# One decoder layer on one core: the eight sums of query squares issued as one run, and the first weights moved to the queue that loads x

## The chip, the cores and the metric

The kernel runs on one core of a Trainium2 chip. The metric is device time in microseconds (us) of one execution, as the median of several runs. TensorE (PE in the rows) does the matmuls, VectorE (DVE) and ScalarE (ACT) the elementwise work, GpSimd (POOL) a little of it, and SyncE (SP) issues most of the DMAs. Times inside a profile count from the start of its span.

## The reference, cut to what matters

One layer of a hybrid decoder for 256 prompt tokens and 8 sampled tokens (264 columns in all), in float32:

```
proj = rms_norm(x, g_mix) @ w_in            # [q | k | v | z | xBC | dt]
q    = rms_norm per head of 64 (q, q_norm_g)
attn = sliding-window attention with sinks (q, k, v)
ssd  = Mamba-2 scan of xBC, dt, gated by silu(z)
x    = x + concat(attn, ssd) @ w_out
x    = x + cross-attention into 256 memory tokens
x    = x + ConvFFN(x)
```

For the change two pieces matter. The first is the opening: the first columns of `w_in` (k and v) times x, for which x (2048 features, 16 blocks of 128) and the weights must be loaded. The second is the norm of the queries: for 16 heads of 64 and 256 prompt tokens the sum of the squares over each head's 64 features.

## The kernel before, in words

Activations lie with features on the 128 partitions and the 264 tokens along the free axis. A projection is done in three matmuls per block of 128 features (lines 100 to 102): weights and activations are each split into a high part, rounded to the matmul's format, and a low remainder, and high x high, high x low and low x high are added in PSUM. The high parts are made by ScalarE (line 85 for weights), the low ones by VectorE (line 86). Each such matmul streams 264 (or 256) columns and is called a wide matmul here.

**The opening** (lines 187 to 261) is ordered by hand on SP, TensorE, ScalarE and VectorE. x and the first 512 weight columns come interleaved, block by block: a block k is 264 columns of x and 512 columns of weights. Block 0 comes in two DMAs, `open_x` (x of block 0 with the gain, 140 KB, issued by SP) and `open_w` (its weights, 256 KB, issued by ScalarE), then SP issues blocks 1 to 5 as one DMA each (388 KB) and blocks 6 to 15 two by two (776 KB). While these fly, TensorE does warm-up matmuls on zeros (line 201). For block 0, ScalarE makes the high part of x (line 161), VectorE and ScalarE each cast one half of the weights (lines 180, 181), VectorE makes the low part of x (line 165) and then that of the weights (line 184). TensorE does 12 matmuls a block (line 240): 4 column groups with high weights and high x, 4 with high weights and low x, 4 with low weights and high x. At the end of the opening come the matmuls for dt, 16 of 32 output columns (line 247), four column groups side by side.

**The query squares** (lines 601 to 631). The queries come out of four projections of two blocks each, eight blocks `qT[:, j]` in all. As each is ready, ScalarE squares it (line 611). Then eight matmuls with 32 output columns (line 615) sum the squares over each head: for d = 0, 1 and j = 0 to 3, block 4d + j adds into the partitions 32j to 32j + 31 of one PSUM bank `pq`, with a stationary matrix `nw[:, d]` that holds ones in the column of each head. The accumulation starts at d = 0 and stops at d = 1. In the profile each of these float32 matmuls is two passes. VectorE copies `pq` (line 628), TensorE transposes it, and from it the reciprocal norms of the queries are made for the attention.

Outside the opening, the order of instructions on each engine is worked out when the kernel is built, from estimated times and dependencies, with earlier lines first where several could go; `tc.high_priority()` puts some ahead, and `tc.issue_after(ins)` keeps the instructions of its block behind `ins` on the same engine. So the eight sums are set among the wide matmuls of the projections as their squares come free.

Of the kernel before, what the change touches and what calls it, by code (L numbers as in the profile page):

```python
# [16 lines left out]
TP, TS = 256, 8  # L17
T = TP + TS
# [29 lines left out]
def hybrid_decoder_step_kernel(ctx: ExitStack, tc: tile.TileContext, I, O):  # L48
    nc = tc.nc
    V, S, P, PE = nc.vector, nc.scalar, nc.gpsimd, nc.tensor  # L50
# [9 lines left out]
    def psum(tag):  # L60
        return ps.tile([128, 512], F32, tag=tag, name=tag, bufs=banks[tag])

    def T3(pool, n, dt=F32, tag=None, name=None, bufs=None):
        return pool.tile([128, n, T], dt, tag=tag, name=name or tag, bufs=bufs)
# [80 lines left out]
    BLK = T + 512  # L145
# [4 lines left out]
    def load(on, src, a, b, k):  # L150

        t = quarter[k // 4]
        o = t.shape[1] - 4 * BLK
        return on.dma_start(out=t[:, o + a:o + b], in_=src)

    def x_of(k):
        return blocks[k // 4][:, k % 4, 0:T], gmix[:, k:k + 1]

    def x_hi(k):
        x, g = x_of(k)  # L160
        return S.activation(out=A[k // 8][0][:, k % 8, :], in_=x, func=AF.Copy, scale=g)

    def x_lo(k):
        x, g = x_of(k)
        return V.scalar_tensor_tensor(out=A[k // 8][1][:, k % 8, :], in0=x, scalar=g, in1=A[k // 8][0][:, k % 8, :].bitcast(F32),
                                      op0=ALU.mult, op1=ALU.subtract)
# [10 lines left out]
    def w_split(k, n, half=False):  # L177
        raw, hi, lo = w_piece(k, n)
        if half:
            V.tensor_copy(out=hi[:, :, 0:256], in_=raw[:, :, 0:256])  # L180
            S.copy(out=hi[:, :, 256:512], in_=raw[:, :, 256:512])
        else:
            S.copy(out=hi, in_=raw)
        return lambda: V.tensor_tensor(out=lo, in0=raw, in1=hi.bitcast(F32), op=ALU.subtract)
# [9 lines left out]
    with tc.manual_schedule(engines={mybir.EngineType.SP, mybir.EngineType.PE, mybir.EngineType.Activation, mybir.EngineType.DVE}):  # L194
        V.memset(acc0, 0.0)
        load(nc.sync, I["open_x"], -KB, T, 0)
        load(S, I["open_w"], T, BLK, 0)

        S.activation(out=table, in_=acc0[:, 0:1], func=AF.Copy)
        for n in (T, T, T, 128):  # L200
            PE.matmul(warm[:, :n], acc0[:, 0:128], acc0[:, 0:n], start=True, stop=True)
        for k in range(1, 6):
            load(nc.sync, I["open_1"][k - 1], BLK * (k % 4), BLK * (k % 4 + 1), k)
        for k in range(6, KB, 2):
            load(nc.sync, I["open_2"][k // 2 - 3], BLK * (k % 4), BLK * (k % 4 + 2), k)

        squares = iter(range(4))

        def square():
            j = next(squares)  # L210
            S.activation(out=sw[j // 2][:, 4 * (j % 2):4 * (j % 2) + 4, :], in_=blocks[j][:, :, 0:T], func=AF.Square)
            if j % 2:
                w = sw[j // 2]
                V.tensor_tensor(out=w[:, 0:4, :], in0=w[:, 0:4, :], in1=w[:, 4:8, :], op=ALU.add)

        for k in range(6):
            x_hi(k)
            lo = w_split(k, 1, k < 2)
            x_lo(k)
            lo()  # L220
        for k in range(6, KB, 2):
            x_hi(k)
            x_hi(k + 1)
            lo = w_split(k, 2)
            x_lo(k)
            x_lo(k + 1)
            lo()
            if k >= 8:
                square()
        nc.sync.dma_start(out=wdt, in_=I["w_dt"])  # L230
        V.tensor_tensor(out=wdt, in0=wdt, in1=gmix.unsqueeze(2).broadcast_to([128, KB, 32]), op=ALU.mult)
        nc.sync.dma_start(out=cst, in_=I["cst"])
        nc.sync.dma_start(out=par, in_=I["par"])
        last_load = nc.sync.dma_start(out=hcol, in_=I["hcol"])

        def first_k(k, i):

            for x in range(2 - i):
                for c in range(4):
                    PE.matmul(first[c][:, :T], pre[k // 2][i][:, k % 2, c * 128:(c + 1) * 128], A[k // 8][x][:, k % 8, :],  # L240
                              start=k + i + x == 0, stop=k == KB - 1 and i == 1)

        def dt_round(r):

            for j in range(4):
                k = 4 * r + j
                PE.matmul(dt_ps[32 * j:32 * j + 32, :T], wdt[:, k, :], x_of(k)[0], start=r == 0, stop=r == 3)


        for ks in ((0,), (1,), (2,), (3,), (4,), (5,), *((k, k + 1) for k in range(6, KB, 2))):  # L250
            for i in range(2):
                for k in ks:
                    first_k(k, i)

        sq_last = S.activation(out=table, in_=sw[1][:, 7, 0:1], func=AF.Sqrt)
        V.tensor_tensor(out=sw[0][:, 0:4, :], in0=sw[0][:, 0:4, :], in1=sw[1][:, 0:4, :], op=ALU.add)
        V.tensor_tensor(out=sw[0][:, 0:2, :], in0=sw[0][:, 0:2, :], in1=sw[0][:, 2:4, :], op=ALU.add)
        add_last = V.tensor_tensor(out=acc0, in0=sw[0][:, 0, :], in1=sw[0][:, 1, :], op=ALU.add)
        for r in range(4):
            dt_round(r)  # L260
        sum_last = PE.matmul(sum0[:, :T], cst[:, C_ONE:C_ONE + 128], acc0, start=True, stop=True)
# [339 lines left out]
    qsq = [T3(apool, 4, tag="R", name=f"qsq{i}", bufs=4) for i in range(2)]  # L601
    nw = zz[:, :, 512:544]
# [7 lines left out]

            S.activation(out=qsq[j // 4][:, j % 4, :TP], in_=qT[:, j, :TP], func=AF.Square)
    pq = psum("s")
    for d in range(2):
        for j in range(4):
            PE.matmul(pq[32 * j:32 * j + 32, 0:TP], nw[:, d, :], qsq[d][:, j, :TP], start=d == 0, stop=d == 1)
    cpc = mp.tile([128, 24, 8], F32, name="cpc")
    ctmp = mp.tile([128, 2, TP], F32, tag="c", name="ctmp", bufs=2).rearrange("p a b -> p (a b)")[:, :192].rearrange("p (a b) -> p a b", b=8)

# [10 lines left out]
    pq = psum("x")  # L629
# [30 lines left out]
    for j in range(8):  # L660
        if j % 4 == 0:
            second_chunk(j // 4)
        d = 2 * (j // 4)
# [893 lines left out]
def build(shapes):  # L1557

    import concourse.bacc as bacc

    nc = bacc.Bacc("TRN2", target_bir_lowering=False, num_devices=1)
    ins = {n: nc.dram_tensor(f"in_{n}_dram", s, dt, kind="ExternalInput").ap() for n, (s, dt) in shapes.items()}
    outs = {n: nc.dram_tensor(f"out_{n}_dram", s, F32, kind="ExternalOutput").ap() for n, s in _OUTS}
    with tile.TileContext(nc, schedule_with_timeline_sim=True) as tc:
        hybrid_decoder_step_kernel(tc, ins, outs)
    return nc
# [10 lines left out]
```

## Time and profile before

| | us |
|---|---|
| median of 3 runs | 1399.48 (1399.35 to 1400.28) |
| the profiled execution, its own time | 1399.1 |
| its span, first to last instruction | 1396.8 |
| TensorE busy in the span | 1391.8 |
| VectorE busy | 1051.1 |
| ScalarE busy | 769.2 |
| GpSimd busy | 95.9 |

The granted clock of TensorE is full over the whole span. The span is what the views of the trace show; the profiled execution's own time has another 2.3 us around it. A row of a timeline gives the start, the length, the engine (q behind it: an issue by its sequencer), the line, the operation, what it writes and reads, the shape, how many like it follow each other, and in brackets how long the engine idled ahead of it and what ended that.

### The profile page before, as it was taken

The page shows a single profiled execution, that of the slowest core. Times are in us where ns is not written, and L with a number is a line of the kernel's source. Part 1 is how long each engine was busy: PE and PEld are TensorE (multiplying, and loading weights), DVE is VectorE, ACT ScalarE, POOL GpSimd, SP SyncE. Part 2 cuts the span into 40 slices and gives each one's busy share as a digit, 9 for nine tenths or more (in the row PEclk, how much of TensorE's full clock was granted, in tenths as well). Part 3 has the DMA queues.
Part 4 walks back from the last instruction along what each step waited for, and adds up shares of the span by engine and source line. Part 5 has one row for each costly group of instructions (what it writes and reads, how often), then busy time and mean ns, then how long its engine had stood idle before and what let it go on. Part 6 is the DMA issues. An engine that isn't in the chain of part 4 may idle for free.

```text
span 1396.8 us, 29012 instructions
## 1 busy us (share of the span) xinstructions
PE 1391.8 (100%) x11535; PEld 1366.9 (98%) x11535; DVE 1051.1 (75%) x1874; ACT 769.2 (55%) x1255; POOL 95.9 (7%) x286
## 2 busy tenths in 40 slices
PE   9999999999999999999999999999999999999999
PEld 8999999999999999899999999999999999999998
DVE  8879799999997774578777775777577757765654
ACT  7667756556545554566565544554455445543532
POOL 0000011121010000002010000000000000000000
PEclk9999999999999999999999999999999999999999
DMA  7954477777776577675676765676566656655654
GB/s 302 321 162 137 137 218 245 231 242 249 244 220 236 182 240 264 206 249 187 190 254 216 253 210 187 212 248 217 183 212 240 196 183 197 196 181 182 191 184 138
DMA packets 89479, 298.33 MB, mean 214 GB/s; under 512 B 12032, under 2 KB 17152, under 8 KB 88832
## 3 DMA queue, kind: packets, MB, share of 16 engines
q1 hardware_dynamic: 83696, 277.35, 60.9%
q0 software_dynamic: 5504, 18.88, 4.1%
q8 instruction: 90, 1.47, 0.4%
q14 instruction: 45, 0.37, 0.1%
q10 hardware_dynamic: 144, 0.26, 0.1%
HBM read 280.77 MB, written 16.23 MB: 213 GB/s over the span
## 4 chain that ended last, share of the span: by engine, by line
PE 99%; DMA 0%; ACT 0%; DVE 0%; issue 0%
PE mm L100 21%; PE mm L101 21%; PE mm L102 21%; PE t L100 10%; PE t L102 10%; PE t L101 10%; PE t L240 1%; PE y L825 1%; PE t L278 1%; PE y L841 0%; PE mm L240 0%; PE s L240 0%; PE x L278 0%; PE t L559 0%; PE x L1137 0%; DMA open<-in_open_x_dram 0%
## 5 line engine op out<-in xcount | busy, mean ns | idle before, releaser
L85 ACT CAST whi<-wraw 128x1024 fp32r<-128x1024 f32 x440 | 459.7, 1048 | 527.4 <-PE mm L101 277.7
L86 DVE TENSOR_TENSOR wlo<-wraw,whi 128x1024 fp32r<-128x1024 f32 x440 | 540.1, 1229 | 220.6 <-ACT whi L85 216.7
L100 PE MATMUL mm<-x2h,whi 128*128 128x264 f32 x704 | 199.9, 284 | 0.0
L100 PE MATMUL t<-x2h,whi 128*128 128x264 f32 x704 | 199.8, 284 | 0.0
L102 PE MATMUL t<-x2h,wlo 128*128 128x264 f32 x704 | 199.7, 284 | 0.0
L101 PE MATMUL mm<-x2l,whi 128*128 128x264 f32 x704 | 199.6, 284 | 0.0
L101 PE MATMUL t<-x2l,whi 128*128 128x264 f32 x704 | 199.5, 283 | 0.0
L102 PE MATMUL mm<-x2h,wlo 128*128 128x264 f32 x704 | 199.4, 283 | 0.0
L101 PE MATMUL mm<-hl,whi 128*128 128x264 f32 x704 | 198.7, 283 | 0.0
L102 PE MATMUL mm<-hh,wlo 128*128 128x264 f32 x704 | 198.2, 283 | 0.0
L100 PE MATMUL mm<-hh,whi 128*128 128x264 f32 x704 | 197.2, 284 | 0.0
L100 PE MATMUL mm<-xh,whi 128*128 128x264 f32 x576 | 164.7, 287 | 0.0
L101 PE MATMUL mm<-xl,whi 128*128 128x264 f32 x576 | 164.5, 287 | 0.0
L102 PE MATMUL mm<-xh,wlo 128*128 128x264 f32 x576 | 162.8, 287 | 0.0
L101 PEld LDWEIGHTS mm<-x2l,whi 128*128 128x128 f32 x704 | 132.5, 188 | 0.0
L101 PEld LDWEIGHTS t<-x2l,whi 128*128 128x128 f32 x704 | 132.5, 188 | 0.0
L100 PEld LDWEIGHTS t<-x2h,whi 128*128 128x128 f32 x704 | 132.5, 188 | 0.0
L100 PEld LDWEIGHTS mm<-x2h,whi 128*128 128x128 f32 x704 | 132.4, 188 | 0.1
L101 PEld LDWEIGHTS mm<-hl,whi 128*128 128x128 f32 x704 | 132.4, 188 | 0.0
L102 PEld LDWEIGHTS t<-x2h,wlo 128*128 128x128 f32 x704 | 132.2, 188 | 0.0
L102 PEld LDWEIGHTS mm<-x2h,wlo 128*128 128x128 f32 x704 | 132.1, 188 | 0.0
L102 PEld LDWEIGHTS mm<-hh,wlo 128*128 128x128 f32 x704 | 131.9, 188 | 0.0
(506 smaller groups left out, 2951.5 us busy)
## 6 DMA issues: line engine op xcount, KB each, us to landing
wraw<-in_w_up_dram SPq DMA_DIRECT2D x176, 512.0 KB, 4.4
wraw<-in_w_in_dram SPq DMA_DIRECT2D x96, 512.0 KB, 4.7
wraw<-in_w_dn_dram SPq DMA_DIRECT2D x88, 512.0 KB, 4.2
wraw<-in_w_out_dram SPq DMA_DIRECT2D x48, 512.0 KB, 4.3
h<-in_h_dram POOLq DMA_DIRECT2D x32, 256.0 KB, 4.7
hn<-in_h_dram SPq DMA_DIRECT2D x16, 512.0 KB, 5.0
out_state_s_dram<-hn POOLq DMA_DIRECT2D x16, 512.0 KB, 3.8
e<-dram_la SPq DMA_DIRECT2D x16, 256.0 KB, 5.1
```

The source lines that it names most:

```text
L85: S.copy(out=hi, in_=x)
L86: V.tensor_tensor(out=lo, in0=x, in1=hi.bitcast(F32), op=ALU.subtract)
L100: PE.matmul(out, wh, xh, start=start, stop=False)
L101: PE.matmul(out, wh, xl, start=False, stop=False)
L102: return PE.matmul(out, wl, xh, start=False, stop=stop)
L240: PE.matmul(first[c][:, :T], pre[k // 2][i][:, k % 2, c * 128:(c + 1) * 128], A[k // 8][x][:, k % 8, :], start=k + i + x == 0, stop=k == K ...
L278: return PE.transpose(out, in_, cst[0:k, C_ID:C_ID + k])
L825: PE.matmul(y[o:o + 64, (h // 2) * 128:(h // 2) * 128 + 128], xdt[:, h, :], es[h // 4][:, h % 4, :], start=True, stop=True)
```

## The change

The DMA of block 0's weights is issued by SP, between that of x and that of block 1, and no more by ScalarE. The eight sums of squares are issued in another order: first that of d = 1, j = 3 (the last block, whose squares come last), and behind it, by `issue_after`, the other three of d = 1 and then the four of d = 0. The accumulation starts at d = 1 and stops at d = 0.

```diff
         load(nc.sync, I["open_x"], -KB, T, 0)
-        load(S, I["open_w"], T, BLK, 0)
+        load(nc.sync, I["open_w"], T, BLK, 0)
...
     pq = psum("s")
-    for d in range(2):
-        for j in range(4):
-            PE.matmul(pq[32 * j:32 * j + 32, 0:TP], nw[:, d, :], qsq[d][:, j, :TP], start=d == 0, stop=d == 1)
+
+    def q_sums(d, j):
+        return PE.matmul(pq[32 * j:32 * j + 32, 0:TP], nw[:, d, :], qsq[d][:, j, :TP], start=d == 1, stop=d == 0)
+
+
+    with tc.issue_after(q_sums(1, 3).ins):
+        for d in (1, 0):
+            for j in range(4 if d == 0 else 3):
+                q_sums(d, j)
```

## Rows read from the trace of the kernel before

**Rows 1.** The page: busy time of the engines with their share of the span and instructions, and the shares of the chain of work that ended last.
```profile
PE 1391.8 (100%) x11535; PEld 1366.9 (98%) x11535; DVE 1051.1 (75%) x1874; ACT 769.2 (55%) x1255; POOL 95.9 (7%) x286
...
PE 99%; DMA 0%; ACT 0%; DVE 0%; issue 0%
```

**Rows 2.** The waits of TensorE over the whole span: who waited for whom, us in total, times, the longest.
```profile
PE x L201 <- DVE eps L274: 1.2, 1, 1.2
PE t L240 <- ACT xh L161: 0.5, 1, 0.5
```

**Rows 3.** The timeline of TensorE from 4 to 8.3 us: block 0 of the opening and the start of blocks 1 (6.79) and 2 (8.25).
```profile
5.10 0.48 PE L240 MATMUL t<-xh,whi 128*128 128x264 f32 x2 [0.46 <-ACT xh L161]
5.42 0.33 PE L240 MATMUL mm<-xh,whi 128*128 128x264 f32 x1
5.58 0.28 PE L240 MATMUL s<-xh,whi 128*128 128x264 f32 x1
...
6.19 0.51 PE L240 MATMUL t<-xh,wlo 128*128 128x264 f32 x2
6.54 0.29 PE L240 MATMUL mm<-xh,wlo 128*128 128x264 f32 x1
...
6.79 0.40 PE L240 MATMUL t<-xh,whi 128*128 128x264 f32 x2
...
8.25 0.28 PE L240 MATMUL t<-xh,whi 128*128 128x264 f32 x1
```

**Rows 4.** The timeline of ScalarE from 0 to 7.4 us: its issue of the first weights, and blocks 0 and 1.
```profile
0.74 0.41 ACTq L154 DMA_DIRECT2D open<-in_open_w_dram  x1
...
4.49 0.52 ACT L161 ACTIVATE xh<-open 128x264 fp32r<-128x264 f32 x1 [1.82 <-DMA open<-in_open_x_dram]
4.92 0.39 ACT L181 CAST whi<-open 128x256 fp32r<-128x256 f32 x1
5.63 0.52 ACT L161 ACTIVATE xh<-open 128x264 fp32r<-128x264 f32 x1 [0.33 <-DMA open<-in_open_dram]
```

**Rows 5.** The timeline of VectorE from 0 to 7.4 us: block 0 and the first cast of block 1.
```profile
4.66 0.29 DVE L180 CAST whi<-open 128x256 fp32r<-128x256 f32 x1 [3.50 <-DMA open<-in_open_w_dram]
5.04 0.49 DVE L165 SCALAR_TENSOR_TENSOR xl<-open,xh 128x264 fp32r<-128x264 f32 x1
5.45 0.68 DVE L184 TENSOR_TENSOR wlo<-open,whi 128x512 fp32r<-128x512 f32 x1
6.05 0.29 DVE L180 CAST whi<-open 128x256 fp32r<-128x256 f32 x1
```

**Rows 6.** The timeline of SP from the start: its first issues (the second row merges ten).
```profile
0.74 0.39 SPq L154 DMA_DIRECT2D open<-in_open_x_dram  x1
1.19 5.72 SPq L154 DMA_DIRECT2D open<-in_open_dram  x10
```

**Rows 7.** The DMA issues of three short stretches, 0.7 to 1.1, 1.2 to 1.6 (block 1) and 1.66 to 2.08 us (block 2, issued at 1.65): KB each and us from issue to landing. The weights were issued at 0.74, as x was.
```profile
open<-in_open_w_dram ACTq DMA_DIRECT2D x1, 256.0 KB, 3.9
open<-in_open_x_dram SPq DMA_DIRECT2D x1, 140.0 KB, 3.7
...
open<-in_open_dram SPq DMA_DIRECT2D x1, 388.0 KB, 4.4
...
open<-in_open_dram SPq DMA_DIRECT2D x1, 388.0 KB, 4.9
```

**Rows 8.** The timeline of TensorE from 81 to 87.1 us: the three runs of line 615 and the wide matmuls ahead of and behind each.
```profile
81.31 0.28 PE L102 MATMUL mm<-xh,wlo 128*128 128x264 f32 x1
81.52 1.06 PE L615 MATMUL s<-qsq,zz 128*32 128x256 f32 x12
82.51 0.39 PE L100 MATMUL mm<-xh,whi 128*128 128x264 f32 x1
82.74 0.29 PE L101 MATMUL mm<-xl,whi 128*128 128x264 f32 x1
...
83.47 0.28 PE L101 MATMUL mm<-xl,whi 128*128 128x264 f32 x1
83.69 0.62 PE L615 MATMUL s<-qsq,zz 128*32 128x256 f32 x2
...
84.46 0.29 PE L100 MATMUL mm<-xh,whi 128*128 128x264 f32 x1
...
86.04 0.28 PE L101 MATMUL mm<-xl,whi 128*128 128x264 f32 x1
86.25 0.62 PE L615 MATMUL s<-qsq,zz 128*32 128x256 f32 x2
...
87.03 0.28 PE L100 MATMUL mm<-xh,whi 128*128 128x264 f32 x1
```

**Rows 9.** The timeline of TensorE from 28.3 to 31.6 us: the matmuls for dt and what follows them.
```profile
28.78 2.00 PE L247 MATMUL x<-open,wdt 128*32 128x264 f32 x32
30.70 0.71 PE L261 MATMUL y<-acc,cst 128*128 128x264 f32 x2
```

**Rows 10.** The timeline of ScalarE from 76 to 96 us: the squares of the last query block.
```profile
82.74 0.41 ACT L611 ACTIVATE qsq<-attn 128x256 f32<-128x256 f32 x1
```

**Rows 11.** The timeline of VectorE from 76 to 96 us: the work ahead of the copy of the sums, and the copy.
```profile
84.35 1.41 DVE L656 TENSOR_TENSOR qs<-attn,qs 64x512 fp32r<-64x512 f32 x2
86.91 0.42 DVE L628 COPY qn<-s 128x256 f32<-128x256 f32 x1 [1.16 <-PE s L615]
```

## The prediction

> **What bounds the kernel now.** I read the page first: TensorE is busy for the whole span and the chain that ended last is TensorE for 99% of it [rows 1]. Then the list of what TensorE waited for: it has two entries, the warm-up at the start and 0.5 us for the first activations, and none in the 1390 us behind [rows 2]. So from the first real matmul at 5.10 on the end is set by two things alone: when that matmul starts, and how many microseconds of TensorE's stream lie behind it. Work on another engine counts only if it moves one of the two.
>
> Next, how dense the stream is. Block 1 of the opening takes 12 matmuls from 6.79 to 8.25: 1.46, or 0.122 a step. Block 0, the same 12, takes 5.10 to 6.79: 1.69 [rows 3]. The 0.23 over are small holes: the third matmul starts 0.32 after the first (two steps are 0.24), the fourth 0.16 after that, and the ninth and tenth take 0.35 together. They are too short for the list of waits, but nothing later gives them back.
>
> The same reading of the sums of squares: the line has 16 passes (two a sum) in three runs, twelve at 81.52, two at 83.69, two at 86.25 [rows 8]. I price a run by the start of the last wide matmul ahead of it to the start of the second one behind it, less two steps (0.24), since the first wide step behind a run is long too. Twelve: 81.31 to 82.74, 1.43, costs 1.19. Two: 83.47 to 84.46, 0.99, costs 0.75. Two: 86.04 to 87.03, also 0.75. Together 2.69. A sixth of the passes costs nearly two thirds of the large run: what is paid is mostly the way into the 32-column form and back.
>
> **The change part by part: the sums.** The work is the same, eight sums; what goes are two of three ways in and out. For the one run of 16, the row of the dt matmuls, of the same 32-column form, is nearest: 32 passes in 28.78 to 30.70, so 0.060 a pass with four column groups side by side [rows 9]. Sixteen passes at that rate are 0.96. The run of twelve already took 0.99 from its first pass to the next wide matmul, as its last four passes, by the order of the code, belong to two sums and so fill two groups only. So the run of 16 fits in the time of the run of twelve, and I take 1.19. The other end: per pass between the runs of two and of twelve the price rises by (1.19 - 0.75) / 10 = 0.044, so four more passes cost 0.18 and the run 1.37. The saving is 2.69 - 1.19 = **1.50**, or 1.32 at the other end.
>
> The first sum of the run, that of block 7, stands where the last one did in the order. In time it moves forward by what the earlier runs no longer take: 86.25 - 1.19 - 0.75 = 84.31, and by the gain of the other edit. Its squares end at 82.74 + 0.41 = 83.15 [rows 10], so TensorE should not wait, with about 1 us of margin. Behind the run VectorE copies the sums: that copy idled 1.16 for the last one [rows 11]. By the new order the last sum is done by 85.3 or so while VectorE is busy until 85.76, so that idle time should vanish; it is worth nothing, as TensorE waits for nothing VectorE makes there. The seven sums that now come later have no other reader than this copy, and their inputs stay where they are meanwhile.
>
> **The first weights' queue.** Before, ScalarE's queue issued them at 0.74, at the same time as SP issued x; they landed 3.9 and 3.7 later, at 4.64 and 4.47 [rows 7]. Block 1, issued on SP at 1.19 [rows 6], landed at 5.59, and block 2, issued at 1.65, at 6.55. So 388 KB arrive every 0.96 us, about 400 GB/s, while SP issues one every 0.46: transfers, not issues, set the pace. Counted back from block 1 at that pace, x and the weights together (396 KB) are in at 5.59 - 0.96 = 4.63, which is where the weights landed, and x alone (140 KB) would be in 0.63 earlier, at 4.0. In one queue the order is x, weights, block 1. I take 4.0 for x, 4.64 for the weights, 5.6 for block 1. The issues of the weights and of every block move one slot of 0.45 later on SP, covered by that backlog; if the cover is gone the price is rival A. On ScalarE the issue of 0.41 disappears ahead of the table load, which had 1.82 of idle time behind it [rows 4]: nothing.
>
> What this brings is in block 0. Now ScalarE makes x's high part from 4.49 to 5.01 and only then its half of the weights, 4.92 to 5.31 [rows 4]; TensorE starts 0.09 after the former. VectorE's half runs 4.66 to 4.95, its low part of x waits for ScalarE until 5.04, the low weights run 5.45 to 6.13 [rows 5]. With x at 4.0 its high part is ready at 4.55; both halves of the weights start at 4.66, and VectorE's ends at 4.95, ScalarE's at 5.05. TensorE starts at 4.95 + 0.09 = 5.04, its third matmul finds its weights, VectorE's low part of x starts near 4.95 and the low weights end near 6.04. Eight steps from 5.04 are 6.01, so about 0.1 of the last hole stays, and block 1 starts at 5.04 + 1.46 + 0.09 = 6.59 where it was 6.79: **0.20**. Block 1's high parts, 5.63 to 6.15 on ScalarE and 6.05 to 6.34 on VectorE (earlier, as VectorE is free earlier), still come ahead of that.
>
> Its bounds: if the weights landed as x and they had no block beside them and nothing else idled, at 4.3, start and gain move by 0.3 more, to 0.5, and then block 1's landing at 5.6 is the limit. If they land a whole slot later the part loses 0.26 (rival A).
>
> In the Trainium skill, DMA: Bandwidth & Descriptors, section "Issuing engines are not separate DMA queues", a second issuing engine only saves the issue time, and all transfers share the same 16 DMA engines. That speaks against the move: it gives the issue time back and wins no bandwidth. By it the sum would be rival A's; the landing rows, one block per 0.96 against one issue per 0.46, speak for the slot being hidden.
>
> **Sum.** 1.50 + 0.20 = 1.70 off the profiled execution's 1399.1 (span 1396.8 and 2.3 around it): 1397.4. The median of the runs shown is 0.4 above that execution, so I give 1397.8 for a median. About 0.2%, 2.8 us, is what a measurement of this kernel can tell from no change; the forecast lies within it.
>
> **The rivals.** A: the slot is not hidden. SP issues the weights at 1.19 instead of 0.74 and they land at 5.09. VectorE's half ends at 5.40, TensorE starts at 5.49 and block 1 at 5.49 + 1.46 + 0.1 = 7.05, 0.26 later than before. With the sums' 1.50 that is 1.24 off: 1398.2. For it: at the very start there is no backlog yet. Against: x is ahead on the same queue and takes its time on the DMA engines meanwhile.
>
> B: the order of the rest is planned anew. Away from the hand-ordered opening, instruction order is worked out when the kernel is built, from estimated times, and both edits shift these. Then other short runs merge or split somewhere in the following 1300 us, each merge or split worth up to the 0.75 of a lone short run. Two more merges give 1.70 + 1.50 = 3.2 off, 1396.3. For it: there are many such runs; against: most of the order is given by data.
>
> C, the other side: the sums are held back but don't stand together. The edit only says that seven sums come behind block 7's; if the wide matmuls of the next pair get in between, each run of a sum or two pays 0.75 at the place of rows 8. Three runs cost what they do now; from the fourth on the edit costs more than it gave. Five runs, about 4.0, are 1.3 more than 2.69, less the opening's 0.2: 1400.6. All eight alone are 6.0: 3.1 slower, 1402.6. Against: six sums that were free to go together did go as one run [rows 8].
>
> **How the numbers follow.** Forecast, 1397.0 to 1398.1 with its bounds, 0.62. A 0.15. B 0.08. C 0.15, a third of it over 2.8 us. The range leaves out B and the worse part of C: 1396.4 to 1400.2. Faster by over 0.2% (below 1396.7) is B and the edge of the forecast, 0.10; slower 0.05; within it 0.85.
>
> **What would show it.** One row of 16 passes of the sums near 84.1, 1.43 from the wide matmul ahead to the second behind; VectorE's copy without its idle time; the weights issued at 1.19 and 3.4 to 3.5 to landing; TensorE's first real matmul near 5.04 and block 1 near 6.6; a span near 1395.1. A first matmul after 5.3 is A; several rows of the sums are C; changed costs of runs behind 90 us are B.

## The result: slower by 4.5 us

The changed kernel takes 1404.05 us (median of 8 runs, 1402.09 to 1408.83) where the kernel before takes 1399.58 on the same chip (8 runs, 1399.25 to 1400.28): a ratio of 1.0039 [1.0028, 1.0050], or 3.9 to 7.0 us more (the ratio of the two medians alone is 1.0032). The forecast was 1397.8, no change that can be measured, and 1400.2 the upper end of its range. The prediction was wrong, on the side to which it gave 0.05.

The profiled execution of the changed kernel is the longest of its eight, 1408.83 with a span of 1406.9. The spans of the eight go from 1400.1 at a mean granted clock of 1.000 to 1406.9 at 0.996, so a part of the loss comes and goes with the clock; the profile before has 1.000.

**What the profile after shows.** First TensorE's waits, the view that had two entries before [rows 2]. Columns: who waited for whom, us in total, times, the longest.

```profile
PE y L831 <- ACT hp L849: 3.4, 1, 3.4
PE mm L100 <- DVE u L740: 2.0, 1, 2.0
PE x L201 <- DVE eps L274: 1.2, 1, 1.2
PE t L100 <- DVE u L896: 1.0, 1, 1.0
```

Behind the edited place line numbers are six higher than before (831 was 825, 849 was 843, 740 was 734). The warm-up wait is the old one. The three others are new, 6.4 us together, and none lies where the change was made: they end at 207.79 (`u`, line 740), 302.21 and 373.57 (`hp`). All three are of one kind. TensorE wants to write a PSUM bank whose last content another engine has yet to read.

Second, the chain that ended last [rows 1]: TensorE had 99% of it, now it has 93%, with VectorE at 3%.

```profile
PE 1395.9 (99%) x11535; PEld 1370.5 (97%) x11535; DVE 1054.1 (75%) x1874; ACT 768.2 (55%) x1255; POOL 92.0 (7%) x286
...
PE 93%; DVE 3%; DMA 1%; ACT 1%; issue 1%; ACTq 0%; DVEq 0%
```

Third, the clock. Busy time by stretches, of after and then of before; columns: the stretch, its length, busy us and instructions of PE, PEld, DVE, ACT and POOL, the granted clock, the DMA share, GB/s.

```profile
209.00:212.40 3.40, 3.40 (x18) 3.40 (x17) 3.40 (x8) 1.57 (x3) 0.00 (x0) 0.50 0.39 146
...
372.90:379.60 6.70, 6.03 (x30) 5.70 (x31) 6.70 (x12) 2.86 (x8) 0.54 (x1) 0.50 0.67 210
```
```profile
209.00:212.40 3.40, 3.40 (x31) 3.40 (x30) 3.40 (x8) 2.49 (x3) 0.00 (x0) 1.00 0.60 206
...
372.90:379.60 6.70, 6.70 (x58) 6.39 (x58) 6.70 (x13) 2.82 (x6) 0.13 (x1) 1.00 0.81 252
```

Behind the wait of 2.0 and that of 3.4 the clock is at 0.50, the lower of its two levels, for 3.4 and 6.8 us, and TensorE gets through 18 and 30 matmuls where it did 31 and 58. Behind the wait of 1.0, at 302, it stays at 1.00.

That accounts for most of the time of this execution. The 1350th wide matmul (those of the opening counted), near 204 us, starts 1.81 earlier than the 1350th of before; the end comes 10.04 later; so 11.85 are lost between. The waits are 2.01 + 1.00 + 3.40 = 6.41. The half clock, by an estimate, costs half of the time that TensorE works at it: of the 3.4 us all, of the second stretch the 6.0 behind 373.57, so 1.7 + 3.0 = 4.7. Together 11.1; 0.7 is left over. With the waits alone the span would be 1396.8 - 1.8 + 6.4 = 1401.4; the run at a clock of 1.000 has 1400.1. This is the account of the longest of the eight, 10.0 over the profile before. The median is only 4.5 over; the changed kernel has no trace of such an execution, and the nearest is that of run_only below, with one of the two long waits.

**The two edited places.** TensorE in the opening, and at the sums, as [rows 3] and [rows 8]:

```profile
4.46 0.48 PE L240 MATMUL t<-xh,whi 128*128 128x264 f32 x2
...
6.18 0.51 PE L240 MATMUL t<-xh,whi 128*128 128x264 f32 x2
...
7.89 0.40 PE L240 MATMUL t<-xh,whi 128*128 128x264 f32 x2
...
84.94 0.28 PE L102 MATMUL mm<-xh,wlo 128*128 128x264 f32 x1
85.15 1.07 PE L615 MATMUL s<-qsq,zz 128*32 128x256 f32 x16
86.15 0.40 PE L100 MATMUL mm<-xh,whi 128*128 128x264 f32 x1
86.39 0.28 PE L101 MATMUL mm<-xl,whi 128*128 128x264 f32 x1
```

Blocks 0, 1 and 2 start 0.64, 0.61 and 0.36 earlier than in the trace before. The sums are one run of 16; from 84.94 to 86.39 is 1.45, so by the price rule of the prediction it costs 1.21 in place of 2.69. On VectorE the copy follows the work ahead of it without idle time, where it idled 1.16 [rows 11]:

```profile
85.43 1.23 DVE L86 TENSOR_TENSOR wlo<-wraw,whi 128x1024 fp32r<-128x1024 f32 x1
86.57 0.42 DVE L634 COPY qn<-s 128x256 f32<-128x256 f32 x1
```

The x of block 0 and its weights, issued by SP at 0.74 and 1.19, landed 2.3 and 2.8 us later, at 3.03 and 4.00 (3.7 and 3.9 from issue before [rows 7]):

```profile
open<-in_open_x_dram SPq DMA_DIRECT2D x1, 140.0 KB, 2.3
...
open<-in_open_w_dram SPq DMA_DIRECT2D x1, 256.0 KB, 2.8
```

So the sums did locally what was forecast for them. The lead in the opening is no proof for the other edit. In the five later traces that keep the weights on ScalarE's queue, with the opening of the kernel before, x landed at 3.42 to 3.95, the weights at 3.63 to 4.13, and TensorE started at 4.29 to 4.59. From run_kept_order:

```profile
4.29 0.79 PE L240 MATMUL t<-xh,whi 128*128 128x264 f32 x2
```

So the one trace before, with its start at 5.10, was late by chance. The matmuls of this row and those behind it stand 0.22 apart until 5.9 and 0.12 from there on. 0.22 is the spacing in the stretches at 0.50, so the clock seems to have been at the lower level there, though the view of the clock, which gives 1.00, does not show it. What is lost is lost 120 to 290 us later.

**How the longest wait comes about.** ScalarE near 373, and TensorE in the same stretch, after:

```profile
364.43 1.28 ACT L815 ACTIVATE e<-e,la 128x128 f32<-128x128 f32 x4 [4.17 <-DMA e<-dram_la]
...
367.64 2.04 ACT L93 CAST ath<-attn 128x1056 fp32r<-128x1056 f32 x2
369.59 1.04 ACT L85 CAST whi<-wraw 128x1024 fp32r<-128x1024 f32 x1
370.53 0.62 ACT L816 ACTIVATE e<-e 128x512 f32<-128x512 f32 x1
371.06 1.98 ACT L85 CAST whi<-wraw 128x1024 fp32r<-128x1024 f32 x2
372.94 0.57 ACT L849 COPY hp<-y 128x512 f32<-128x512 f32 x1
```
```profile
369.15 1.02 PE L847 MATMUL y<-xw,Bn 128*128 128x512 f32 x2
373.57 1.12 PE L831 MATMUL y<-e,xdt 128*64 128x128 f32 x8 [3.40 <-ACT hp L849]
```

And the same two engines before:

```profile
369.25 0.59 ACT L843 COPY hp<-y 128x512 f32<-128x512 f32 x1 [0.17 <-PE y L841]
```
```profile
368.19 1.02 PE L841 MATMUL y<-xw,Bn 128*128 128x512 f32 x2
...
372.07 0.66 PE L825 MATMUL y<-e,xdt 128*64 128x128 f32 x8
```

The matmuls into y have one bank. Before, ScalarE's copy `hp` stood right behind the matmuls that fill it, and TensorE did wide matmuls until 372.07. After, the copy stands behind five casts and an exponential, and on TensorE the next user of the bank stands directly behind the last one. ScalarE works without pause from 364.43, but in its order: the copy starts at 372.94 though its input was done by 370.2. The Trainium skill says so too: in "PSUM — Partial Sum Buffer", section "Engine vs sequencer instructions", ScalarE's and VectorE's queues are strictly first in, first out; the trace agrees.

The copy is not alone in being late. By the code the last four of the eight matmuls into y also read VectorE's product of line 817, which comes behind ScalarE's exponential of line 816 and other work of VectorE:

```profile
373.39 0.67 DVE L817 TENSOR_TENSOR e<-e,s 128x512 f32<-128x512 f32 x1
```

With the copy early and this product where it is, those four would still have waited. So new_hp_early, below, moves both, and only kept_hp_late tells what the copy does by itself.

At 207 it is VectorE: the product of line 740, which reads an `mm` bank of PSUM, starts at 207.31, behind a subtraction of 1.22 us and two shorter rows that new_u_early, below, puts behind it; before, it started at 205.88.

```profile
206.17 1.22 DVE L86 TENSOR_TENSOR wlo<-wraw,whi 128x1024 fp32r<-128x1024 f32 x1
207.31 0.43 DVE L740 TENSOR_TENSOR u<-mm,r 128x264 f32<-128x264 f32 x1
```

### The profile page after: what moved, and what is told of

It is laid out like the page before. It is cut to its first block, busy times and chain, and to the rows that moved or that the text cites. A ratio compares the mean times of both kernels' runs of the same rounds, so it can differ in the third digit from the quotient of the medians.

```text
span 1406.9 us, 29014 instructions
## 1 busy us (share of the span) xinstructions
PE 1395.9 (99%) x11535; PEld 1370.5 (97%) x11535; DVE 1054.1 (75%) x1874; ACT 768.2 (55%) x1255; POOL 92.0 (7%) x286
## 4 chain that ended last, share of the span: by engine, by line
PE 93%; DVE 3%; DMA 1%; ACT 1%; issue 1%; ACTq 0%; DVEq 0%
PE mm L100 20%; PE mm L101 20%; PE mm L102 20%; PE t L100 9%; PE t L101 9%; PE t L102 9%; DVE wlo L86 1%; PE t L240 1%; PE t L278 1%; PE y L831 1%; DMA h<-in_h_dram 0%; DMA e<-dram_la 0%; PE mm L240 0%; PE s L240 0%; DVE ych L876 0%
```

## The experiments

**Theory.** The run edit makes the instruction order be planned anew when the kernel is built, and the new order has these waits; the edits by themselves are worth what was predicted. **Rivals:** the queue edit does it (a DMA late somewhere), or the run itself does, through what holding the sums back shifts in time.

The orders in the traces already say how far the edits reach, as far as line, names and shape tell instructions apart. With the queue edit alone every engine's order is that of before but for the moved DMA. With the run edit alone it is that of the changed kernel but for that DMA. Against before, the changed kernel has another instruction at 1514 places of TensorE's order, 571 of VectorE's, 242 of ScalarE's and some of GpSimd's and SyncE's. All of these lie between 82 and 418 us; behind that the orders are the same.

To take order and edit apart, some kernels hold an order fixed: a list of trace positions per engine, and an issue-order edge (no wait) from each instruction to the next. In the trace of run_kept_order, below, VectorE, ScalarE and SyncE have the order of before, and TensorE's differs only where the sums stand.

```diff
+    _keep_order(tc)                     # last line of the kernel
...
+def _keep_order(tc):
+    traced = tc.nc.cur_bb.bb.instructions
+    for at in ORDER.values():           # per engine
+        for a, b in zip(at, at[1:]):
+            tc.add_manual_dep(traced[b], traced[a].name, NoSync, ...)
```

All ratios below are to the kernel before on the same chip, whose medians were 1399.30 (queue_only, run_only, run_kept_order, both_kept_order) and 1399.33 on each of two others (the four kernels with moved instructions; order_only and the three taken again). The medians are of 11 runs, of 5 for run_only, order_only and new_u_early.

**queue_only**, the queue edit alone:

```diff
-        load(S, I["open_w"], T, BLK, 0)
+        load(nc.sync, I["open_w"], T, BLK, 0)
```

> The first weights on SP's queue alone; the sums stay in three runs, and the instruction order of all engines is that of the kernel before. Theory (the opening gains, the loss comes from the new instruction order that the other edit brings): TensorE starts near 4.5 and block 2 of the opening 0.36 us earlier than before, as in the changed kernel's trace, no wait of TensorE behind the opening, granted clock full: 1399.6 - 0.4 = 1399.2, 0.1 to 0.6 faster. Rival (the queue edit makes the loss, by loads that come late all along): 1402 or more and waits of TensorE behind 200 us.

1399.26 us, ratio 1.0001 [0.9992, 1.0010]; taken again as **queue_only_again**:

> The queue edit alone once more, on one chip with the next two. Theory (it starts TensorE 0.6 us earlier, and the landing of blocks 1 and 2 takes that back): within 0.4 of the kernel before. Rival (it makes the landing of block 2 later): 0.5 or more slower than before.

1399.09, 0.9998 [0.9989, 1.0007]. No wait behind the warm-up in the first trace, whose first matmul is 0.66 earlier than in the trace before (and not earlier than in run_kept_order's). The 150th wide matmul behind the opening is 0.24 earlier there and 0.10 later in the second. So the rival that blames the queue falls, and the edit's own worth is nothing that shows.

**run_only**, the run edit alone (the second hunk of the change):

> The sums in one run alone, the weights on ScalarE's queue; the instruction order, worked out anew at build, is that of the changed kernel on every engine but for the moved DMA. Theory (new order): as slow as the changed kernel or 0.4 more, 1402 to 1409 from run to run, with waits of TensorE near 208, 302 and 373 us and a halved clock behind the long ones. Rival (the queue edit makes the loss): 1399.6 - 1.5 = 1398.1.

1403.68, ratio 1.0034 [1.0021, 1.0046]. The wait for `hp` is there at 3.0, with half clock behind it from 370.2 to 373.6. The loss belongs to the run edit. Not yet told: the sums, or the order?

**run_kept_order**, the eight sums as one run at the last one's place, all else held in the order of before, the weights on ScalarE's queue:

> The sums in one run, the weights on ScalarE's queue, and every other instruction of every engine held by explicit edges in the order of the kernel before; the eight sums stand where the last one stood. Theory (the run is worth 1.5 and only the new order loses): 1399.6 - 1.5 = 1398.1, no wait of TensorE behind the opening, full clock. Rival (the run itself, TensorE arriving 1.5 us earlier at everything behind it, brings the waits): 1402 or more, waits near 200 to 375 us with this order too.

1397.66, ratio 0.9989 [0.9980, 0.9997]; again as **run_kept_again**:

> The sums in one run with the old order once more: 1.5 faster than the kernel before (1.3 to 1.8), the best version of the study.

1397.83, 0.9988 [0.9980, 0.9997]. TensorE's only wait in the first is the warm-up's. The sums and the copy behind them, from TensorE's and VectorE's timelines:

```profile
83.85 0.28 PE L101 MATMUL mm<-xl,whi 128*128 128x264 f32 x1
84.06 1.07 PE L615 MATMUL s<-qsq,zz 128*32 128x256 f32 x16
85.07 0.39 PE L102 MATMUL mm<-xh,wlo 128*128 128x264 f32 x1
85.30 0.28 PE L100 MATMUL mm<-xh,whi 128*128 128x264 f32 x1
```
```profile
85.44 0.41 DVE L628 COPY qn<-s 128x256 f32<-128x256 f32 x1
```

83.85 to 85.30 is 1.45, a cost of 1.21 and a saving of 1.48. Timed, it is 1.64 and 1.50 less than before. The run is worth what was predicted, and the second rival falls. From this kernel to run_only it is 6.02 us, with the same sums in one run and the weights on the same queue; only the order differs.

**order_only**, neither edit: the sums in three runs as before, everything else held in the order of the changed kernel:

> Neither edit: the sums in three runs (six, one, one, with 8 and 15 wide matmuls between them as before), the weights on ScalarE's queue; every other instruction of every engine is held in the order of the changed kernel. Theory (the new order alone loses about 6): 1403.7 + 1.5 = 1405.2, 1403 to 1407, the wait of TensorE near 371 us there. Rival (the new order loses only because TensorE, with the sums in one run, arrives 1.5 us earlier at VectorE's and ScalarE's work): 1401 or less, the wait shorter by 1.5.

1406.44, ratio 1.0052 [1.0040, 1.0065]: 7.1 us for the order alone. Its waits of TensorE, and the stretch at half clock (columns as above):

```profile
PE y L825 <- ACT hp L843: 3.4, 1, 3.4
PE x L201 <- DVE eps L274: 1.2, 1, 1.2
PE x L278 <- DVE xw L820: 0.6, 1, 0.6
PE t L100 <- DVE u L890: 0.4, 1, 0.4
PE t L240 <- ACT whi L183: 0.3, 1, 0.3
PE mm L100 <- DVE u L734: 0.3, 1, 0.3
```
```profile
373.40:376.80 3.40, 3.40 (x18) 3.40 (x17) 3.40 (x5) 1.23 (x4) 0.54 (x1) 0.50 0.82 241
```

The longest wait is the changed kernel's, to the place. Order 7.1, less the run's 1.50 to 1.64, is 5.5 to 5.6, inside the 3.9 to 7.0 measured for the change.

**both_kept_order**, both edits, the order of before held:

> Both edits, and every other instruction of every engine held by explicit edges in the order of the kernel before. Theory: the two gains add, 1399.6 - 1.5 - 0.4 = 1397.7, no waits of TensorE behind the opening. Rival (TensorE, almost 2 us earlier, runs into VectorE and ScalarE whatever the order): a wait of 1 us or more somewhere from 200 to 400 us and 1400 or more.

1398.23, ratio 0.9994 [0.9985, 1.0003]; again as **both_kept_again**:

> Both edits with the old order once more: as the kernel above within 0.4 if the queue edit is worth nothing, 0.5 or more slower if it makes block 2 late, 0.3 or more faster if the opening's gain lasts.

1397.98, 0.9991 [0.9982, 0.9999]. With the queue edit it is 0.57 and 0.15 slower than without it, inside the intervals. So the two gains that were expected to add did not: the queue edit gave none. The opening of the first (ScalarE, then TensorE):

```profile
7.37 0.52 ACT L161 ACTIVATE xh<-open 128x264 fp32r<-128x264 f32 x1 [1.02 <-DMA open<-in_open_dram]
```
```profile
4.43 0.49 PE L240 MATMUL t<-xh,whi 128*128 128x264 f32 x2
...
8.45 0.51 PE L240 MATMUL t<-xh,whi 128*128 128x264 f32 x2 [0.47 <-ACT whi L183]
```

TensorE starts 0.67 earlier than in the trace before but 0.14 later than in run_kept_order's, and block 2 lands at 7.35 (6.53 there), so that TensorE waits 0.47. Block 2 landed between 6.53 and 7.71 with the weights on ScalarE's queue and between 6.58 and 8.05 with them on SP's, over all traces: late landings occur with either.

**new_hp_early**, the changed kernel with its own order held but for three instructions near 373: the exponential of line 816 moved ahead of the squares at 365.62, the copy `hp` right behind the cast at 369.59, and VectorE's product of line 817 ahead of its two subtractions (line 93) at 369.24:

```diff
-ACT: e L815, squares.., ath L93 x2, whi, e L816, whi x2, hp L849
+ACT: e L815, e L816, squares.., ath L93 x2, whi, hp L849, whi x2
```

> The changed kernel with its own order held by explicit edges, but for three instructions near 373 us: ScalarE's second half of the decay (e, the exponential) directly behind its first half, ScalarE's copy that frees the y bank ahead of two weight casts instead of behind them, and VectorE's product with e ahead of the two low parts of the attention output. Theory (TensorE waits there because that copy stands behind 2 us of casts and one late exponential): the wait of 3.0 to 3.4 becomes 1 or less and the halved clock behind it goes: 2.3 + 1.7 to 3.4 less than the changed kernel, 1399 to 1400. Rival (TensorE is held by the total of work on ScalarE and VectorE there, not by these places): the wait only moves, 1403 to 1404.

1401.44, ratio 1.0019 [1.0010, 1.0028]. The wait for `hp` shrinks from 3.4 to 1.0, another of 0.5 appears beside it, and the clock stays whole from 365 to 382. Three instructions take back about half of the loss; 1399 to 1400 was expected.

**new_u_early**, the changed kernel's order with one instruction on VectorE, the product of line 740 at 207.31, moved ahead of line 753 at 204.97:

```diff
-DVE: xs L753, ych L876, wlo L86, u L740
+DVE: u L740, xs L753, ych L876, wlo L86
```

> The changed kernel with its own order held by explicit edges, but for one instruction: VectorE's evacuation of a projection's bank at 207.3 us stands in front of the three instructions that were ahead of it (from 204.97 on). Theory: the wait of TensorE at 207.8, 2.0 in the changed kernel's trace and none in the trace of the sums alone, does not come, nor the halved clock behind it; the wait at 373 stays. Median 1402 to 1403.5, and runs as slow as 1408 no more. Rival (the place does not matter): 1404, 1402 to 1409 from run to run.

1405.24, ratio 1.0042 [1.0030, 1.0055]. The wait at 207 is gone, the one for `hp` is 3.4 as before, with 6.8 us at half clock behind it. In the trace the end is 2.7 earlier than in the profile after; in the median nothing is gained, against what the removed wait of 2.0 should give. The expectation, 1402 to 1403.5, was missed, and the median is the rival's. Why stays open; the changed kernel itself spreads from 1402.09 to 1408.83, and these five lie at 1404.0 to 1406.2.

**new_three_moves**, both of these and the product of line 896 at 301.64 moved ahead of line 86 at 300.01:

> The changed kernel with its own order held by explicit edges, with the moves of the two kernels beside it, and the evacuation at 301.6 us one weight product earlier. Theory: no wait of TensorE of over 1 us is left behind the opening, the clock stays full, 1397.7 to 1399.0, which is the time of the old order with both edits (1398.2) within 0.8. Rival (other waits come up in the new order): 1400 or more.

1400.51, ratio 1.0013 [1.0004, 1.0022]. Its waits:

```profile
PE x L201 <- DVE eps L274: 1.2, 1, 1.2
PE y L831 <- ACT hp L849: 1.0, 1, 1.0
PE mm L100 <- ACT ath L93: 0.5, 1, 0.5
PE t L240 <- ACT whi L183: 0.5, 1, 0.5
PE t L240 <- ACT whi L181: 0.2, 1, 0.2
```

From the changed kernel's 4.5 over before it is 1.2 over; the kernel with both edits and the old order is 1.1 to 1.4 under. Of the 2.3 to 2.5 that remain, 1.5 are the waits of 1.0 and 0.5, at 368.0 and 365.6. The waits in the opening, 0.7, explain little of the rest, as the traces of the other two kernels have 0.5 and 0.6 there. So 0.8 to 1.0 is open, and 1397.7 to 1399.0 was expected: three moves do not make the new order as good as the old.

**kept_hp_late**, the reverse: run_kept_order with the one ScalarE copy `hp` moved from 369.25 to behind the instruction at 373.89, seven places later:

> The sums in one run, weights on ScalarE's queue, the order of the kernel before held, but for one instruction: ScalarE's copy that frees the y bank (369.25 us in the trace before) stands behind the seven instructions that followed it there, so that it ends near 373.2 instead of 368.1. Theory: the next y matmuls of TensorE, at 370.4 in that order, wait about 2.9, and the clock is halved for 3 to 7 us behind that: 1397.7 + 2.9 + 1.5 to 3.4 = 1402.1 to 1404.0. Rival (a wait costs its own length only): 1400.6; or nothing, if the wait is made up later: 1397.7.

1401.76, ratio 1.0016 [1.0007, 1.0025]; 4.1 above run_kept_order's 1397.66, or 3.8 by the two ratios, as the two ran on different chips. ScalarE's copy, TensorE's row and the clock behind it:

```profile
373.23 0.56 ACT L843 COPY hp<-y 128x512 f32<-128x512 f32 x1
```
```profile
373.85 1.12 PE L825 MATMUL y<-e,xdt 128*64 128x128 f32 x8 [2.75 <-ACT hp L843]
```
```profile
373.80:377.20 3.40, 3.35 (x18) 3.02 (x19) 3.40 (x8) 0.00 (x0) 0.00 (x0) 0.51 0.78 199
```

A wait of 2.75 and half of 3.4 us are 4.45; measured 3.8 to 4.1, a little under what was expected and more than the wait by itself. One copy in the wrong place, and nothing else moved, brings a wait and a half clock of the changed kernel's kind into a kernel that has neither.

## Why the prediction was wrong, step by step

- **The run of 16.** Right: 1.21 in place of 2.69, a saving of 1.48 by the trace against 1.50 forecast. Of the two ends, 1.50 and 1.32, the chosen one held. VectorE's idle time ahead of the copy went, as said.
- **The opening.** The weights were issued at 1.19, as forecast, but the term of 0.20 was reckoned from one execution that was not typical. Over the traces x lands at 2.91 to 3.03 with the edit and 3.42 to 4.47 without, the weights at 3.93 to 4.54 with it and 3.63 to 4.13 without (4.63 in the trace before alone). So x gains, the weights, for which TensorE has to wait, do not, and its first matmul comes at 4.39 to 5.00 with the edit and 4.29 to 5.10 without. The slot is not hidden either: block 1, issued 0.46 later, lands at 5.28 to 5.98 with the edit, without it at 4.78 to 5.09 in five of six traces. Rival A's 0.26 does not show all the same: TensorE comes to block 1 at 6.10 to 6.94 with the edit, 6.14 to 6.79 without. Forecast 0.20, measured 0.0 and 0.2 alone, each plus or minus 1.3: the size is within the noise, the mechanism is not borne out. The Trainium skill, "DMA: Bandwidth & Descriptors", section "Issuing engines are not separate DMA queues", says that a second issuing engine saves only issue time. The timed runs agree with it in so far as moving the issue moved nothing (1.0001 and 0.9998).
- **The failed step is rival B.** It named the cause, the order planned anew, but priced it only by short runs that merge or split, "each merge or split worth up to the 0.75 of a lone short run", as a gain to 1396.3, with a chance of 0.08, "most of the order is given by data" as the reason against. Measured, the order alone costs 7.1. Data fixes what must come before what; it left free which ready instruction ScalarE takes while a PSUM bank waits for its copy.
- **What lay under it.** "TensorE waits for nothing VectorE makes there" and "work on another engine counts only if it moves one of the two" were read from a trace with no waits behind the opening [rows 2]. That is a property of that order, not of the kernel. With VectorE 75% busy and a single bank for y, it holds only while each copy out of PSUM stands early enough.
- **Rival C** did not come about: all 16 passes stand together. It was the only slower case, so the range ended at 1400.2.
- The last step to look at, "changed costs of runs behind 90 us are B", looked for runs. It should have looked at waits, of which there had been none.

## What to carry to other kernels

Where a planner works out the order when the kernel is built, a constraint on eight instructions can reorder hundreds of microseconds of work behind them, and the price of the order is drawn anew: here 7.1 us lost against 1.5 gained. Compare the built orders of the two versions before believing a sum of local terms, and ask of each PSUM bank with one buffer who copies it out and what stands ahead of that copy on its engine. Do not take the rows of one trace as the kernel's where the executions spread: the opening's term rested on one late landing. Hold the order and make the edit alone, and it is worth its sum: the best version here is run_kept_order at 1397.7, ratio 0.9989 [0.9980, 0.9997].

## What the runs showed beyond the question

- **The clock behind a wait.** Waits of TensorE of 2.0, 2.75, 3.0 and 3.4 us in mid-kernel each came with a granted clock of 0.50 for 3.4 us, and in two traces for about 6.8; waits of 1.0 and 0.5 did not. The wait of 2.75 cost 3.8 to 4.1 in all. In the two traces with 6.8 (after and new_u_early) the clock fell 0.8 and 0.5 us before the wait ended, in the others at its end or up to 1.2 behind it, so the same wait of 3.4 cost more in one than in another. What decides when it falls is open.
- **Late packets.** Block 2 landed anywhere from 6.53 to 8.05. In seven of the ten traces where it landed behind 7.0, single packets of the blocks took 1.2 to 2.1 us where the median is 0.12, by the trace's packet records; in one of the ten, run_kept_again at 7.71, none took 0.9. So late packets are not all of it, and why is open.
- **Why the plan went wrong** is argued, not shown. ScalarE idles 4.17 for the load of `e` ahead of its late stretch, which suggests that the load is reckoned to land earlier than it does. But in the kernel before it idles up to 5.1 for the same load without cost to TensorE, so that alone does not settle it. A change of those estimates was not tried.
